# Cached K of an attention layer laid out in DRAM during the layer before it, and loaded in one transfer of 8 KB rows

## The chip, the cores and the metric

The kernel runs on one core of one Trainium2 chip. A core has a matrix engine (TensorE, PE in the profile, with PEld for its weight loads), a vector engine (VectorE, DVE), a scalar engine (ScalarE, ACT), a general engine (GpSimd, POOL) and a sync engine (SyncE, SP) that here issues nearly all DMAs. Each engine runs its instructions in the order in which they stand in its own queue, and waits at an instruction until what it needs is there. The core has 16 DMA engines, an on-chip memory of 128 partitions (SBUF) and eight accumulation banks (PSUM) of 128 x 512 floats. The metric is the device time of one execution in microseconds (us), as the median of several runs.

## What is computed

Two transformer-like layers over 512 prompt tokens and 8 x 16 sample tokens (640 in all), in float32. Layer 0 is a gated MLP with a spatial mix over blocks of 128 tokens, layer 1 is an attention with 16 heads of width 128 and a forget bias. The 8 sample sequences of layer 1 also attend to 256 cached rows each, which come as `cache_fox_k` and `cache_fox_v` in DRAM. Cut to that:

```python
for i in range(2):
    hp, hs = rms_norm(xp, norm_pre[i]), rms_norm(xs, norm_pre[i])
    if i == 0:                       # gated MLP: u, v, z = h @ w_in (1024 x 6144)
        ...                          # y = gelu(u) * (w_s mixes layer_norm(gelu(v))) * silu(z); y @ w_out
    else:                            # q, k, v, z, logf = h @ w_in (1024 x 8208)
        op = (fox_attend_prompt(qp, kp, vp, lfp) * silu(zp)) @ fox_w_out
        att_s = fox_attend_sample(qs, ks_, vs_, lfs, cache_fox_k, cache_fox_v, cache_fox_logf)
        os_ = (att_s * silu(zs)) @ fox_w_out
    xp, xs = xp + rms_norm(op, norm_post[i]), xs + rms_norm(os_, norm_post[i])
    ...                              # gated embedding input added to xp and xs

def fox_attend_sample(q, k_new, v_new, logf_new, k_cache, v_cache, logf_cache):
    k = jnp.concatenate([k_cache, k_new], axis=1)          # (8, 256 + 16, 16, 128)
    v = jnp.concatenate([v_cache, v_new], axis=1)
    s = jnp.einsum('bqhd,bkhd->bhqk', q, k) * scale        # + forget bias, causal mask, softmax
    return jnp.einsum('bhqk,bkhd->bqhd', p, v)
```

`cache_fox_k` holds 8 x 256 x 16 x 128 floats (16.8 MB).

## The kernel before, in words

**Precision.** Each float32 product is made of three passes of the matrix engine. `split` (L261) makes a high part on ACT (L263) and a low part on DVE (L264); `mm3` (L247) issues high x high, high x low and low x high (L249 to L251). Every weight and every activation goes through such a split.

**Weights.** A list of units of 512 KB each is fetched in order by SP into a ring of three buffers, `RAW` (and in part of layer 0 a fourth one in `R1`). `weights` (L224) and `prefetch` (L201) split units into the ring `W`, which has five places, as far ahead as places are free. A fetch waits until the split of the unit that used its buffer is done, and a split waits until PE is done with the place in `W`.

**Layer 0.** First four panels of the v part (L434): sixteen units, each for 30 matmuls of 512 columns. Then eight pairs of channel groups (L588), g = 0, 2, ... 14. For each pair `seven_products` (L523) runs twice, for u and for z. It forms a 2 x 2 block product with seven block products in place of eight; POOL prepares sums of weights (L198), DVE and ACT add up the seven results out of four PSUM banks (L528, L536 to L543), ACT and DVE apply gelu and the gate (L578, L582, L583). At the end of a pair `gate_spatial` (L557) mixes v along the tokens (L565, L566) and multiplies (L568, L570, L573), and then calls `spatial_weights` (L494) for the group two further on. That issues three small loads of 64 KB each: the mixing matrix `w_s` (L497), its bias `b_s` copied to all partitions (L498), and a row of sums `rs_sc` (L499), written once to DRAM before. The bias and the sums go into buffers that the group two before has just been reading, so they can be issued only when L568 and L570 of that group are done. L500 on DVE combines these two loads as soon as they are there; its result is first read by L568 of that later group. Layer 0 ends with `tail` (L602): 16 units of the output product, then the embedding.

**Layer 1.** For each of 8 head pairs p the projections v, k, q, z (L846 to L894) run on PE, and pieces of the attention of the pair before are put between them by `interleave` (L328), which takes a list of (due time, piece) and issues a piece when the sum of the projection steps reaches its due time. The cached rows are handled in 16 sets (p, bg), bg being the half of the 8 sample sequences. `load_k` (L974) loads one set of cached K: 8 DMAs of 128 KB that bring rows of 32 floats (128 bytes) so that each of four partition quarters holds 32 x 32 blocks. `turn_k` (L987) then transposes these blocks on DVE (L992, eight instructions) into `kt`, and `scores` (L1009) multiplies them (L1014). Set (p, 1) is loaded at due time 2 of a pair and set (p + 1, 0) in the middle of it; the transposes of a set come some 22 us later. One buffer of 1 MB (`o_K` in `r2b_t`) takes all sets in turn.

**What sets the order.** A scheduler places the instructions of each engine from the program order, the data they wait for and its own estimate of times; `queued` (L122) asks that what follows be issued right behind a given instruction. So an added DMA can also move instructions on DVE, ACT and PE.

Of the kernel before, what the change touches and what calls it, by code (L numbers as in the profile page):

```python
# [17 lines left out]
F32 = mybir.dt.float32  # L18
# [6 lines left out]
P = 128  # L25
# [32 lines left out]
def hybrid_trunk(tc, x_prompt, x_sample, ck, cv, clf, p_prompt, p_sample, norm_pre, norm_post,  # L58
# [25 lines left out]
    x_sc = dram.tile([NT, P, D], F32, name="x_sc")  # L84
    y_sc = dram.tile([H, P, TOK], F32, name="y_sc")
    c_sc = dram.tile([H, SEQ], F32, name="c_sc")
    cs_sc = dram.tile([P, 272], F32, name="cs_sc")
    rs_sc = dram.tile([16, P], F32, name="rs_sc")

# [28 lines left out]
    def dma(out, in_):  # L118
        behind["sp"] = nc.sync.dma_start(out=out, in_=in_)
# [104 lines left out]
    def weights(n):  # L224

        i0 = state["used"]
        state["used"] += n
        prefetch(i0 + 2 * NW, i0)
        res = []
        for i in range(i0, i0 + n):  # L230
            u, j = items[i]
            k, o, m = units[u][1], place[i][0] * 1024, len(place[i]) * 512
            if j in (1, 2):
                views = [W[:, o + z:o + z + m].rearrange("p (a k n) -> p k a n", a=2, k=k) for z in (0, m)]
            else:
                views = [W[:, o + z:o + z + m].rearrange("p (k n) -> p k n", k=k) for z in (0, m)]
            res.append(tuple(views))
        return res
# [8 lines left out]
    def mm3(out, lhs, rhs, start, stop):  # L247
        (lh, ll), (rh, rl) = lhs, rhs
        nc.tensor.matmul(out, lh, rh, start=start, stop=False)  # L249
        nc.tensor.matmul(out, lh, rl, start=False, stop=False)  # L250
        nc.tensor.matmul(out, ll, rh, start=False, stop=stop)  # L251
# [50 lines left out]
    def h_at(k, a, b):  # L302
        return h_hi[:, k, a:b], h_lo[:, k, a:b]
# [38 lines left out]
    def r2(o, n, p=P):  # L342
        return R2[:p, o:o + n]
# [64 lines left out]
                split(*right_sum(dst), o)  # L408


    def v_at(p, t):
        return r1(p * 2560 + t * 512, 512)

# [20 lines left out]
    for p in range(4):  # L434
        if p == 2:
            with queued("act", "dve", "sp"):
                spatial_constants()
        out = [bank((0, 1, 2, 3, 4, 5, 6, 7)) for _ in range(NT)]
        for kk in range(4):
            (w,) = weights(1)  # L440
            for t in range(NT):
                for j in range(2):
                    k = 2 * kk + j
                    mm3(out[t], h_at(k, t * P, (t + 1) * P), (w[0][:, j], w[1][:, j]), k == 0, k == 7)
            if (p, kk) == (1, 1):
                with queued("act", "dve"):
                    right_operands()
            if (p, kk) == (3, 1):
                split(*quarter(0, 1), b12)
        for t in range(NT):  # L450
            behind["act"] = nc.scalar.activation(out=v_at(p, t), in_=out[t], func=AF.Gelu_apprx_tanh)
            behind["dve"] = nc.vector.bn_stats(out=stats[t][:, 6 * p:6 * p + 6], in_=v_at(p, t))
# [58 lines left out]
    def uv_of(g):  # L511
        return r1(o_u + (g % 2) * TOK, TOK), r1(o_tz + (g % 2) * TOK, TOK)
# [10 lines left out]
    def seven_products(into, done):  # L523

        rights = (quarter(0, 0), right_sum(1), quarter(0, 1), right_sum(0), quarter(1, 1), quarter(1, 0), right_sum(2))

        def total(i, j, a, b):
            nc.vector.tensor_tensor(out=into(i, j), in0=a, in1=b, op=ALU.add)  # L528
            done(i, j, into(i, j))

        for n, (w, right) in enumerate(zip(seven_left(), rights)):
            o = bank(UZ)[:, :HT]
            for k in range(4):
                mm3(o, (w[0][:, k], w[1][:, k]), (right[0][:, k], right[1][:, k]), k == 0, k == 3)
            if n == 0:
                nc.scalar.activation(out=m1, in_=o, func=AF.Copy)  # L536
            elif n == 1:
                nc.vector.tensor_tensor(out=u2, in0=m1, in1=o, op=ALU.add)  # L538
            elif n == 2:
                nc.vector.tensor_tensor(out=u3, in0=u2, in1=o, op=ALU.add)  # L540
            elif n == 3:
                total(1, 1, u3, o)
                nc.vector.tensor_tensor(out=u2, in0=u2, in1=o, op=ALU.add)  # L543
            elif n == 4:
                total(0, 1, u2, o)
            elif n == 5:
                total(0, 0, m1, o)
            else:
                total(1, 0, u3, o)
# [38 lines left out]
    for g in range(0, 16, 2):  # L588
        for part, finish in ((0, finish_u), (1, finish_z)):
            if 2 * part in SEVEN:  # L590
                seven_products(lambda i, j: uv_of(g + i)[part][:, HALF[j]], lambda i, j, c: finish(g, i, j, c))
            else:
                eight_products(lambda i, j, c: finish(g, i, j, c))
        if g < 6:

            with queued("act", "dve"):
                layer_norm_panel(1 + g // 2)
        for i in range(2):
            gate_spatial(g + i)


    def tail(layer, y_at, first_banks, attention=None):  # L602
# [3 lines left out]
        last = layer == 1  # L606
# [39 lines left out]
        def out_steps(h, kks):  # L646
            out = [PB[i] for i in halves[h]]
            for kk in kks:
                (w,) = weights(1)

                split_y(min(2 * kk + 4, 14) if attention and h == 0 and kk < 7 else 16 * h + 2 * kk + 6)
                if h == 1 and kk == 2 and last:
                    embedding_input((2, 3, 4))
                if h == 1 and kk == 5:
                    for t in range(NT):
                        dma(x1[t], tok_rows(xin_p, xin_s, t) if not last else x_sc[t])
                for t in range(NT):
                    for j in range(2):
                        g = 2 * kk + j
                        i, ts = 16 * h + g, slice(t * P, (t + 1) * P)  # L660
                        mm3(out[t], (y_part(i, 0)[:, ts], y_part(i, 1)[:, ts]), (w[0][:, j], w[1][:, j]), g == 0, g == 15)
                    yield 1.36
# [95 lines left out]
    n = NT * H  # L758
# [207 lines left out]
    def kv_of(p, bg):  # L966

        i = 2 * p + bg
        kr = r2(o_K, 2048).rearrange("p (h b n) -> p h b n", h=2, b=4)
        kt = r2(o_KT, 2176).rearrange("p (h b k) -> p h b k", h=2, b=4)  # L970
        vv = [r2(o_V + (2 * i + z) % 3 * 1024, 1024).rearrange("p (b t n) -> p b t n", b=2, t=2) for z in range(2)]
        return kr, kt, vv

    def load_k(p, bg):  # L974
        kr, _, _ = kv_of(p, bg)
        for hh in range(2):
            for qd in range(4):
                d = slice(qd * 32, (qd + 1) * 32)
                dma(kr[d, hh].rearrange("p b (c d) -> p (b c) d", d=32),
                    ck[0, 4 * bg:4 * bg + 4, :, 2 * p + hh, d].rearrange("b (c j) d -> j (b c) d", j=32))  # L980

    def load_v(p, bg):
        for z, vv in enumerate(kv_of(p, bg)[2]):
# [161 lines left out]
```

## Time and profile before

| | |
|---|---|
| median of 3 runs | 1334.27 us (1334.1 to 1334.35) |
| the profiled execution | 1334.83 us, of which 1333.0 us is the span of the profile |
| granted PE clock | 0.999 |
| busy time of PE | 1321.0 us |
| busy time of DVE, ACT, POOL | 766.4, 542.9, 135.7 us |
| moved by DMA | 172.87 MB in 299913 packets, 188769 of them under 512 bytes |
| share of DMA engine time in use | 0.3 to 0.4 from 67 to 540 us, 0.7 to 0.8 from 540 to 1100 us |

The profile is of one execution. A busy PE means that matmuls follow each other without a gap that the records show; the ends of matmuls are modelled, so two matmuls in a row overlap in the records. "Idle before" is the time in which an engine had nothing to run, with the instruction or DMA that ended it. The chain of waits follows the last instruction back to what released it, and so on to the start. Rows with SPq are DMA issues: the time is that of the issue, not of the transfer.

Layer 0 runs to about 457 us (panels to 126 us, the pairs of groups to 347 us, then the output product), the embedding and the norm to about 540 us, layer 1 to the end, its attention part to about 1190 us.

### The profile page before, as it was taken

The page shows a single profiled execution, that of the slowest core. Times are in us where ns is not written, and L with a number is a line of the kernel's source. Part 1 is how long each engine was busy: PE and PEld are TensorE (multiplying, and loading weights), DVE is VectorE, ACT ScalarE, POOL GpSimd, SP SyncE. Part 2 cuts the span into 40 slices and gives each one's busy share as a digit, 9 for nine tenths or more (in the row PEclk, how much of TensorE's full clock was granted, in tenths as well). Part 3 has the DMA queues.
Part 4 walks back from the last instruction along what each step waited for, and adds up shares of the span by engine and source line. Part 5 has one row for each costly group of instructions (what it writes and reads, how often), then busy time and mean ns, then how long its engine had stood idle before and what let it go on. Part 6 is the DMA issues. An engine that isn't in the chain of part 4 may idle for free.

```text
span 1333.0 us, 21550 instructions
## 1 busy us (share of the span) xinstructions
PE 1321.0 (99%) x8363; PEld 1191.6 (89%) x8363; DVE 766.4 (57%) x1581; ACT 542.9 (41%) x1025; POOL 135.7 (10%) x144
## 2 busy tenths in 40 slices
PE   9999999999999999999999999999999999999998
PEld 6888999999988788999999999999999998888786
DVE  7744899998844546544545454444545465544642
ACT  5434555444535334523433333433334344435341
POOL 1013444543000100000000000000000000000100
PEclk9999999999999999999999999999999999999999
DMA  6432334232324204688778575778778687243211
GB/s 224 138 100 70 120 114 130 66 109 68 127 95 158 78 18 127 178 142 158 138 154 176 145 163 141 164 144 163 125 151 169 152 212 235 101 149 111 64 64 47
DMA packets 299913, 172.87 MB, mean 130 GB/s; under 512 B 188769, under 2 KB 269201, under 8 KB 299810
## 3 DMA queue, kind: packets, MB, share of 16 engines
q1 hardware_dynamic: 299666, 171.23, 51.7%
q8 instruction: 65, 1.06, 0.3%
q14 instruction: 38, 0.31, 0.1%
q10 hardware_dynamic: 144, 0.26, 0.1%
HBM read 149.86 MB, written 21.59 MB: 129 GB/s over the span
## 4 chain that ended last, share of the span: by engine, by line
PE 94%; DVE 3%; issue 1%; ACT 1%; DMA 0%; POOL 0%; SPq 0%; DVEq 0%
PE pb L249 28%; PE pb L251 27%; PE pb L250 27%; PE pb L960 3%; PE pb L953 1%; PE pb L1014 1%; PE pb L1040 1%; PE pb L287 1%; DVE W L264 1%; PE pb L565 1%; PE pb L1037 1%; DVE R L583 0%; DMA RAW<-in_gmlp_w_in 0%; PE pb L1032 0%; DVE R L528 0%
## 5 line engine op out<-in xcount | busy, mean ns | idle before, releaser
L249 PE MATMUL pb<-A,W 128*128 128x384 f32 (+2 forms) x1024 | 330.2, 322 | 2.1 <-DVE R L538 1.8
L251 PE MATMUL pb<-A,W 128*128 128x384 f32 (+2 forms) x1024 | 317.1, 310 | 0.0
L250 PE MATMUL pb<-A,W 128*128 128x384 f32 (+2 forms) x1024 | 316.6, 309 | 0.0
L249 PE MATMUL pb<-W,A 128*128 128x512 f32 (+1 forms) x840 | 298.3, 355 | 2.1 <-ACT R L686 1.4
L251 PE MATMUL pb<-W,A 128*128 128x512 f32 (+1 forms) x840 | 293.7, 351 | 0.6 <-DVE A L264 0.6
L250 PE MATMUL pb<-W,A 128*128 128x512 f32 (+1 forms) x840 | 294.0, 350 | 0.0
L264 DVE TENSOR_TENSOR W<-RAW,W 128x1024 fp32r<-128x1024 f32 (+1 forms) x156 | 194.0, 1244 | 139.7 <-ACT W L263 137.5
L263 ACT ACTIVATE W<-RAW 128x1024 fp32r<-128x1024 f32 (+1 forms) x156 | 161.1, 1033 | 156.8 <-PE pb L250 65.1
L249 PEld LDWEIGHTS pb<-A,W 128*128 128x128 f32 x1024 | 193.0, 188 | 10.9 <-issue 6.8
L250 PEld LDWEIGHTS pb<-A,W 128*128 128x128 f32 x1024 | 193.0, 189 | 0.6
L251 PEld LDWEIGHTS pb<-A,W 128*128 128x128 f32 x1024 | 192.6, 188 | 0.4 <-issue 0.4
L249 PEld LDWEIGHTS pb<-W,A 128*128 128x128 f32 x840 | 159.1, 189 | 26.4 <-issue 3.1
L251 PEld LDWEIGHTS pb<-W,A 128*128 128x128 f32 x840 | 158.9, 189 | 21.1 <-DVE A L264 0.9
L250 PEld LDWEIGHTS pb<-W,A 128*128 128x128 f32 x840 | 159.0, 189 | 20.4 <-issue 0.4
L264 DVE TENSOR_TENSOR A<-R,A 128x640 fp32r<-128x640 f32 (+1 forms) x51 | 41.0, 835 | 74.1 <-ACT A L263 71.9
L992 DVE STREAM_TRANSPOSE r2b_t<-r2b_t 128x256 f32<-128x256 f32 x128 | 46.4, 413 | 33.9 <-PE pb L1014 26.2
L263 ACT ACTIVATE A<-R 128x640 fp32r<-128x640 f32 (+1 forms) x51 | 36.6, 746 | 67.7 <-PE pb L250 65.7
L249 PE MATMUL pb<-tb,W 128*128 128x320 f32 x192 | 59.8, 312 | 0.1
L251 PE MATMUL pb<-tb,W 128*128 128x320 f32 x192 | 59.5, 310 | 0.0
L250 PE MATMUL pb<-tb,W 128*128 128x320 f32 x192 | 59.5, 310 | 0.0
L273 POOL TENSOR_TENSOR SML<-SML 128x1 f32<-128x1 f32 x25 | 18.1, 724 | 385.1 <-DVE SML L271 380.5
L955 ACT ACTIVATE R<-pb 128x128 f32<-128x128 f32 (+1 forms) x64 | 27.9, 436 | 65.7 <-PE pb L953 65.4
(235 smaller groups left out, 1866.7 us busy)
## 6 DMA issues: line engine op xcount, KB each, us to landing
RAW<-in_fox_w_in SPq DMA_DIRECT2D x64, 512.0 KB
RAW<-in_gmlp_w_in SPq DMA_DIRECT2D x40, 512.0 KB
r2b_t<-in_cache_fox_v SPq DMA_DIRECT2D x32, 512.0 KB
r2b_t<-in_cache_fox_k SPq DMA_DIRECT2D x128, 128.0 KB
RAW<-in_gmlp_w_out SPq DMA_DIRECT2D x16, 512.0 KB
RAW<-in_ple_w_gate SPq DMA_DIRECT2D x16, 512.0 KB
RAW<-in_fox_w_out SPq DMA_DIRECT2D x16, 512.0 KB
out<-R SPq DMA_DIRECT2D x40, 128.0 KB
```

Source lines behind the costliest of these rows:

```text
L249: nc.tensor.matmul(out, lh, rh, start=start, stop=False)
L250: nc.tensor.matmul(out, lh, rl, start=False, stop=False)
L251: nc.tensor.matmul(out, ll, rh, start=False, stop=stop)
L263: nc.scalar.activation(out=hi, in_=src, func=AF.Copy)
L264: nc.vector.tensor_tensor(out=lo, in0=src, in1=f(hi), op=ALU.subtract)
L273: nc.gpsimd.tensor_tensor(out=q, in0=t, in1=mhalf, op=ALU.pow)
L287: nc.tensor.transpose(out=b[:, j * P:(j + 1) * P], in_=src[:, (4 * c + j) * P:(4 * c + j + 1) * P], identity=ident)
L565: nc.tensor.matmul(b0[:, t * P:(t + 1) * P], v_at(pnl, t)[:, c0:c0 + P], wm, start=True, stop=True)
L953: nc.tensor.transpose(out=tb[:, j * P:(j + 1) * P], in_=pr[:, j * P:(j + 1) * P], identity=ident)
L955: nc.scalar.activation(out=pt[:, :n], in_=tb[:, :n], func=AF.Copy)
L960: nc.tensor.matmul(O[:, d], v[:, j, hh * P:(hh + 1) * P], pt[:, j * P:(j + 1) * P], start=(j == 0), stop=(j == i))
L992: nc.vector.transpose(out=kt[:, hh, bl, :PAST], in_=kr[:, hh, bl])
```

## The change

A DRAM buffer `kc_sc` of 16 sets of 1 MB is added. During layer 0, 128 DMAs copy the cached K from DRAM to this DRAM buffer in the order in which the transposes want it: each is one of the old 128 KB loads with its 128-byte pieces, but with DRAM as the target. They are issued on SP right behind the last DMA issued at that place: two behind each of the 16 weight units of the panels, four behind each of the 16 calls of `seven_products`, two behind each of the 16 units of the output product. In layer 1 `load_k` becomes one DMA of 1 MB, 128 rows of 8 KB, in place of eight of 128 KB.

```diff
+    kc_sc = dram.tile([16, P, 2048], F32, name="kc_sc")
...
+    laid = iter([(p, bg, hh, qd) for p in range(8) for bg in range(2) for hh in range(2) for qd in range(4)])
+
+    def lay_k(n):
+        with queued("sp"):
+            for _ in range(n):
+                p, bg, hh, qd = next(laid)
+                d = slice(qd * 32, (qd + 1) * 32)
+                dma(kc_sc[2 * p + bg, d, hh * 1024:(hh + 1) * 1024].rearrange("j (n d) -> j n d", d=32),
+                    ck[0, 4 * bg:4 * bg + 4, :, 2 * p + hh, d].rearrange("b (c j) d -> j (b c) d", j=32))
...                                   # panels, in the loop over the units
+            lay_k(2)
...                                   # pairs of groups, once for u and once for z
                 seven_products(lambda i, j: uv_of(g + i)[part][:, HALF[j]], lambda i, j, c: finish(g, i, j, c))
+                lay_k(4)
...                                   # output product of layer 0, in the loop over the units
+                if not last:
+                    lay_k(2)
...
     def load_k(p, bg):
-        kr, _, _ = kv_of(p, bg)
-        for hh in range(2):
-            for qd in range(4):
-                d = slice(qd * 32, (qd + 1) * 32)
-                dma(kr[d, hh].rearrange("p b (c d) -> p (b c) d", d=32),
-                    ck[0, 4 * bg:4 * bg + 4, :, 2 * p + hh, d].rearrange("b (c j) d -> j (b c) d", j=32))
+        dma(r2(o_K, 2048), kc_sc[2 * p + bg])
```

Lines of the changed kernel stand 1 lower up to L410 of before, 13 lower in `spatial_weights`, `seven_products` and `gate_spatial` (L500 is L513 there, L538 is L551, L540 is L553, L568 is L581).

How the instructions stand, first on SP in the middle of layer 0, where the pair g = 2, 3 ends and the loads for groups 4 and 5 are issued. Before (`RAW` is a weight fetch; `in_gmlp_b_s`, `rs_sc` and `in_gmlp_w_s` are the three small loads of `spatial_weights`):

```order
L119 DMA sf<-rs_sc 128x128
L119 DMA R_69<-in_gmlp_w_s 128x128
L119 DMA RAW<-in_gmlp_w_in 128x4x256 x2
L119 DMA R_69<-in_gmlp_b_s 128x128
L119 DMA R_69<-rs_sc 128x128
L119 DMA R_69<-in_gmlp_w_s 128x128
L119 DMA R_69<-in_gmlp_b_s 128x128
```

The same place now:

```order
L120 DMA sf<-rs_sc 128x128
L120 DMA R_69<-in_gmlp_w_s 128x128
L120 DMA RAW<-in_gmlp_w_in 128x4x256
L120 DMA kc_sc<-in_cache_fox_k 32x32x32 x4
L120 DMA RAW<-in_gmlp_w_in 128x4x256
L120 DMA R_69<-in_gmlp_b_s 128x128 x2
L120 DMA R_69<-rs_sc 128x128
```

Four copies now stand between the two weight fetches, ahead of both bias loads and of the sums. One pair later (end of g = 4, 5) it is alike: two weight fetches and then four copies stand ahead of the bias load for group 7, which stood ahead of the fetches before, and of the bias load and the sums for group 8. And again at the end of g = 6, 7 and the middle of the next pair, for groups 9 and 10, before

```order
L119 DMA R_69<-rs_sc 128x128
L119 DMA R_69<-in_gmlp_b_s 128x128
L119 DMA RAW<-in_gmlp_w_in 128x4x256 x2
L119 DMA R_69<-in_gmlp_w_s 128x128
L119 DMA sf<-rs_sc 128x128
L119 DMA R_69<-in_gmlp_b_s 128x128
```

and now:

```order
L120 DMA R_69<-rs_sc 128x128
L120 DMA R_69<-in_gmlp_b_s 128x128
L120 DMA RAW<-in_gmlp_w_in 128x4x256 x2
L120 DMA kc_sc<-in_cache_fox_k 32x32x32 x4
L120 DMA R_69<-in_gmlp_b_s 128x128
L120 DMA sf<-rs_sc 128x128
```

The last two loads, for group 10, stand behind the four copies here.

On DVE the scheduler has put L500 (now L513) a few instructions later in most of these places. At the first of the three, before (`W<-sf`, `W<-R` are low parts of splits, `pb` are PSUM banks):

```order
L264 TENSOR_TENSOR W<-sf,W 128x1024
L500 SCALAR_TENSOR_TENSOR sf<-sf,SML,R_69 128x128
L568 SCALAR_TENSOR_TENSOR R_69<-pb_76,SML,sf 128x4x128
L500 SCALAR_TENSOR_TENSOR R_69<-R_69,SML 128x128
L264 TENSOR_TENSOR W<-R_69,W 128x512
L538 TENSOR_TENSOR R_69<-R_69,pb_72 128x320
L540 TENSOR_TENSOR R_69<-R_69,pb_73 128x320
```

and now:

```order
L265 TENSOR_TENSOR W<-sf,W 128x1024
L265 TENSOR_TENSOR W<-R_69,W 128x512
L551 TENSOR_TENSOR R_69<-R_69,pb_72 128x320
L513 SCALAR_TENSOR_TENSOR sf<-sf,SML,R_69 128x128
L513 SCALAR_TENSOR_TENSOR R_69<-R_69,SML 128x128
L553 TENSOR_TENSOR R_69<-R_69,pb_73 128x320
```

A split and L538 moved ahead of the two L500, and L568 between them moved away to a later place. The order on PE changes only in layer 0, where some two dozen matmuls, most of them of the spatial mix, move past their neighbours; in layer 1 it is the same as before.

## The prediction

> **What bounds the kernel now.** I read the page first, then busy time by stretches, the waits of PE, the chain of waits, and the timelines of DVE and SP where the chain leaves PE.
>
> ```profile
> PE 1321.0 (99%) x8363; PEld 1191.6 (89%) x8363; DVE 766.4 (57%) x1581; ACT 542.9 (41%) x1025; POOL 135.7 (10%) x144
> ```
>
> PE is idle for 12 us in the whole span. By stretches (columns: length, busy time of PE, PEld, DVE, ACT, POOL, clock, share of the DMA engines' time, GB/s):
>
> ```profile
> 540.00:610.00 70.00, 70.00 (x498) 66.43 (x497) 29.35 (x56) 24.86 (x43) 3.45 (x6) 1.00 0.82 162
> 610.00:800.00 190.00, 190.00 (x1473) 180.14 (x1472) 95.99 (x302) 69.76 (x160) 5.30 (x18) 1.00 0.76 155
> 800.00:1000.00 200.00, 200.00 (x1544) 189.88 (x1543) 94.17 (x284) 73.44 (x165) 4.58 (x15) 1.00 0.73 148
> ```
>
> Where the cached K is loaded today the DMA engines work at 0.73 to 0.82 of their time, but PE is busy in all of it. The waits of PE between 540 and 1212 us have no row at all. So no transfer of layer 1 ends a wait of PE, and a shorter or earlier one has nothing to give back there.
>
> Layer 0 is different in its pairs of groups:
>
> ```profile
> 177.00:200.00 23.00, 23.00 (x161) 22.53 (x160) 22.72 (x34) 11.78 (x24) 11.17 (x7) 1.00 0.34 101
> 200.00:222.00 22.00, 21.59 (x149) 21.15 (x148) 20.09 (x31) 13.23 (x23) 8.11 (x6) 1.00 0.35 108
> 222.00:259.00 37.00, 36.26 (x248) 35.62 (x247) 34.24 (x52) 16.67 (x31) 18.07 (x11) 1.00 0.35 106
> 259.00:277.00 18.00, 17.01 (x120) 16.82 (x118) 17.33 (x25) 8.82 (x16) 7.85 (x5) 1.00 0.26 81
> ```
>
> DVE is busy 22.72 of 23 us and 17.33 of 18 us, as full as PE. The chain of waits in order of time (start, length, what) says which of the two binds:
>
> ```profile
> 177.61 0.48 DVE R L540
> ...
> 181.35 1.84 DVE W L264
> ...
> 200.53 0.48 DVE R L528
> ...
> 259.34 1.45 issue
> ...
> 275.92 0.74 DVE R L559
> ```
>
> From 177.6 to 201 us and from 259 to 277 us it runs mostly over DVE. The waits of PE between 166 and 300 us name the link, L538, which empties a PSUM bank that PE needs:
>
> ```profile
> PE pb L249 <- DVE R L538: 1.8, 2, 1.1
> ```
>
> So **layer 1 is bound by PE alone, and from 177 to 277 us layer 0 has DVE and PE both full**, with next to no reserve between them. Here the change puts its copies.
>
> **What it removes in layer 1: nothing on the path.** 128 loads go, each holding SP for 562 ns at the median:
>
> ```profile
> L119 SPq DMA_DIRECT2D r2b_t<-in_cache_fox_k x128: 317/562/3949, 567.7 to 1090.0; - x128
> ```
>
> Only DVE waited for them visibly, in two places (L992; us in all, times, longest):
>
> ```profile
> DVE r2b_t L992 <- DMA r2b_t<-in_cache_fox_k: 6.3, 2, 3.8
> ```
>
> DVE has half its time free there (95.99 of 190 us busy). Gain: 0. The 1 MB load that takes their place must wait for all eight transposes of the set before, not for four, and lands as a whole. At the 155 GB/s of this stretch it takes 1.05 MB / 155 = 6.8 us, and the transposes come some 22 due-time us later. The first set, which is transposed at 574 us today, moves to about 585 us in the order. Cost: 0, covered by those 22 us; if the cover went, DVE would wait with half its time free.
>
> **What it adds in layer 0.** A copy from DRAM to DRAM is not in the trace. The nearest rows are 128-byte loads from DRAM and 128-byte stores to DRAM (the K rows of the new tokens):
>
> ```profile
> 570.00:572.00 2.00, 2.00 (x9) 0.67 (x7) 0.36 (x1) 0.00 (x0) 0.00 (x0) 1.00 0.98 148
> 573.80:575.20 1.40, 1.40 (x12) 1.40 (x11) 1.02 (x3) 0.76 (x1) 0.00 (x0) 1.00 0.56 82
> ```
>
> The first is mostly loads: 148 / 0.98 = 151 GB/s with the engines full, so 131072 B take 0.87 us. The second is all stores: 82 / 0.56 = 146 GB/s, 0.90 us. A copy reads and writes such pieces. If both sides overlap it costs 0.87 us, if one follows the other 1.77 us; from below, 0, if it fits wholly into gaps. I take 0.87 us, the nearest row, and a group of four as **3.5 us**, and keep 0 and 7 us for the range.
>
> In the panels and in the output product two copies (1.7 us) come per weight unit, and a unit is 30 matmuls, by the count below 30 x 33.00 / 149 = 6.6 us of PE. The stretch, then SP's waits (fetches wait for buffers, not for the transfer):
>
> ```profile
> 34.00:67.00 33.00, 33.00 (x149) 27.31 (x148) 25.74 (x22) 13.27 (x15) 0.23 (x2) 1.00 0.47 143
> ```
>
> ```profile
> SPq L119 <- DVE W L264: 316.0, 75, 31.1
> ```
>
> ACT's waits show only five for a fetch of layer 0's w_in; its timeline has the first and the last of them within 20 us, for the first five fetches, and in the new order all copies stand behind these:
>
> ```profile
> ACT W L263 <- DMA RAW<-in_gmlp_w_in: 5.7, 5, 3.5
> ```
>
> ```profile
> 7.70 1.06 ACT L263 ACTIVATE W<-RAW 128x1024 fp32r<-128x1024 f32 x1 [3.52 <-DMA RAW<-in_gmlp_w_in]
> ...
> 19.64 1.06 ACT L263 ACTIVATE W<-RAW 128x1024 fp32r<-128x1024 f32 x1 [0.19 <-DMA RAW<-in_gmlp_w_in]
> ```
>
> Cost: 0, covered by the five places of `W` (some 30 us of PE); without that, 1.7 us per unit.
>
> In the pairs of groups the weights are as well covered, but **the small loads are not**. L500 on DVE already waits for them in three places (DVE, with the wait and its cause; then SP):
>
> ```profile
> 175.04 0.35 DVE L500 SCALAR_TENSOR_TENSOR sf<-sf,SML,R 128x128 f32<-128x128 f32 x1 [1.55 <-DMA R<-in_gmlp_b_s]
> 177.61 0.49 DVE L540 TENSOR_TENSOR R<-R,pb 128x320 f32<-128x320 f32 x1
> ...
> 205.84 0.35 DVE L500 SCALAR_TENSOR_TENSOR sf<-sf,SML,R 128x128 f32<-128x128 f32 x1 [1.46 <-DMA sf<-rs_sc]
> 206.72 0.48 DVE L538 TENSOR_TENSOR R<-R,pb 128x320 f32<-128x320 f32 x1
> 207.30 0.49 DVE L540 TENSOR_TENSOR R<-R,pb 128x320 f32<-128x320 f32 x1
> ...
> 234.60 0.35 DVE L500 SCALAR_TENSOR_TENSOR sf<-sf,SML,R 128x128 f32<-128x128 f32 x1 [1.61 <-DMA R<-in_gmlp_b_s]
> 234.87 0.48 DVE L538 TENSOR_TENSOR R<-R,pb 128x320 f32<-128x320 f32 x1
> ...
> 235.86 1.22 DVE L264 TENSOR_TENSOR W<-sf,W 128x1024 fp32r<-128x1024 f32 x1
> ```
>
> ```profile
> 168.11 1.50 SPq L119 DMA_DIRECT2D RAW<-in_gmlp_w_in  x2
> 169.70 0.46 SPq L119 DMA_DIRECT2D R<-in_gmlp_b_s  x1
> ...
> 199.33 0.38 SPq L119 DMA_DIRECT2D RAW<-in_gmlp_w_in  x1
> 202.10 0.33 SPq L119 DMA_DIRECT2D R<-in_gmlp_b_s  x1
> 202.76 0.33 SPq L119 DMA_DIRECT2D sf<-rs_sc  x1
> ...
> 227.68 1.47 SPq L119 DMA_DIRECT2D RAW<-in_gmlp_w_in  x2
> ```
>
> A small load is served behind what was issued before it: alone it is used 205.84 - 202.76 = 3.1 us after its issue, behind two fetches 175.04 - 169.70 = 5.3 us. From the issue of the second fetch (169.2, being 168.11 + 1.50 - 0.38; 228.8 likewise) to the use it is 5.8 us both times. In the new order four copies stand there too, so that the data come 5.8 + 3.5 = 9.3 us after the second fetch. The 2.2 us for which SP issues the copies lie inside that.
>
> - Place 1: data at 169.2 + 9.3 = 178.5; two L500 (0.27 us each, as from 234.60 to 234.87) end at 179.05. L540, next in the new order, started at 177.61: **1.45 us late**. A split and L538 now run ahead of L500, which the waiting hides.
> - Place 2: 199.33 + 9.3 = 208.6; then L500, L538 and L500, some 0.95 us, so L540 at 209.55 and not at 207.30: **2.25 us late**.
> - Place 3: 228.8 + 9.3 = 238.1, L500, then the split at 238.35 and not at 235.86: **2.5 us late**.
>
> At the other L500 of layer 0 the order puts L500 later than 9.3 us behind the second fetch, or no copies stand just ahead. Sum on DVE: 6.2 us. Of that PE is spared what DVE has free. From 200 to 222 us DVE is idle for 1.91 us, 1.46 of it the wait above, so 0.45 is free; from 222 to 259 us 2.76 less 1.61, so 1.15. At place 1 nothing is: the chain runs over DVE right there. So PE ends 1.45 + 1.8 + 1.35 = **4.6 us** later, and nothing after 277 us gives it back, since PE is full. That is 1334.83 + 4.6 = 1339.4 us for the profiled execution, and on the median, 0.56 us lower, **1338.9 us**.
>
> **The Trainium skill against the trace.** "DMA: Bandwidth & Descriptors", section "Why small descriptors are slow (HBM only)", gives each packet about 3 cycles on top of one per 32 bytes; for 128 bytes that makes 4/7 of the 435 GB/s of the section "Where 436 GB/s comes from", an estimate of 249 GB/s, 2.1 us per group of four and by rival 1 below 0.4 us on PE: no change. The load row above, 151 GB/s with the engines full, speaks against it. The section "Specifications" of that page says that below 512 bytes the engine does a read-modify-write, so a write would cost a read too, as in the second rival below. The store row, 146 GB/s, shows no such surcharge on stores from SBUF; no row here shows a write from DRAM.
>
> **The rivals.**
> 1. *The small loads come hardly later, and the new order wins.* Were the copies free, L500 moved behind work that is ready would shed the three waits of 1.55 + 1.46 + 1.61 = 4.6 us; PE could take back at most its idle time from 200 to 277 us, 0.41 + 0.74 + 0.99 = 2.1 us: 1332.2 us. In general DVE loses 3 x (group) less 4.3 us (6.2 at 3.5) and PE 1.6 less. So it turns at a group of 2.0 us, and up to 2.9 us it stays within 0.2% (2.7 us, about what a measurement of this kernel can tell from no change). For it: only 0.35 of the DMA time is used there. Against it: the queue rows.
> 2. *Read and write one after the other:* 7 us per group, 3 x 7 - 4.3 - 1.6 = 15.1 us, 1349 us, and up to 1356 us with three more L500 (160, 276, 300 us) that would then wait. Against it: load and store rows that are alike.
> 3. *Faster, by less traffic in layer 1.* Matmuls of 512 columns took 391 ns on average from 350 to 457 us and 395 ns from 1130 to 1200 us, where more is moved:
>
> ```profile
> L249 PE MATMUL pb<-W,A 128*128 128x512 f32 x157 | 61.4, 391 | 0.0
> ```
>
> ```profile
> L249 PE MATMUL pb<-W,A 128*128 128x512 f32 x83 | 32.8, 395 | 0.0
> ```
>
>  If DMA writes were the cause of that 1%, the 540 us of K loading could win as much at most: 5.4 us, 1328.9 us. Against it: ends of matmuls are modelled, and 4 ns is little.
> 4. *It doesn't do what it says:* a 1 MB load lands late and the transposes wait. DVE has room, so 1334.3 us.
>
> **How the numbers follow.** Forecast (a group of 2.9 to 5 us) 0.50, own range 1337 to 1343; rival 2 0.12; rival 1 with all that stays within 0.2%, and rival 4, together 0.33; rival 3 0.05. That makes slower by over 0.2% 0.62, same 0.33, faster 0.05. The range from 1332.5 (rival 1) to 1349 (rival 2 at its three places) leaves out rival 3 and the upper part of rival 2.
>
> **What would show it.** L513 of the new profile waits about 3 to 4 us for `b_s` or `rs_sc` at the three places, PE's waits for L551 grow from 1.8 to some 6 us between 170 and 280 us, and layer 1 keeps its length. If L513 doesn't wait longer, the copies are cheaper than 0.5 us each; waits of 7 us would mean the double price. A shorter layer 1 with a full PE would show rival 3; new waits of PE after 570 us for transposes, rival 4.

## The result, and the profile after

| | before | after |
|---|---|---|
| median (4 runs each, the same chip) | 1334.19 us (1334.1 to 1334.35) | 1342.91 us (1342.27 to 1343.39) |
| the profiled execution, its span | 1334.83, 1333.0 us | 1342.27, 1340.5 us |

The ratio is 1.0063, with a 95% interval of 1.0051 to 1.0076: 8.7 us slower, where 4.6 were forecast. The busy times of the page of after are almost those of before:

```profile
PE 1322.6 (99%) x8363; PEld 1191.6 (89%) x8363; DVE 765.5 (57%) x1581; ACT 542.3 (40%) x1025; POOL 133.4 (10%) x144
```

PE works 1.6 us longer and is idle for 18 us in place of 12. Layer 1 (windows, columns as in the prediction) moves about as many GB/s in less DMA time, with PE as full as before:

```profile
610.00:800.00 190.00, 190.00 (x1475) 180.14 (x1475) 92.97 (x284) 71.36 (x159) 3.72 (x16) 1.00 0.60 150
800.00:1000.00 200.00, 200.00 (x1540) 190.92 (x1539) 96.83 (x297) 72.13 (x163) 3.94 (x17) 1.00 0.61 152
```

The share of DMA time falls from 0.76 and 0.73 to 0.60 and 0.61, and nobody gains by it. The lost time lies in the pairs of groups. DVE's waits there from 120 to 350 us (us, times, longest):

```profile
DVE R L513 <- DMA R<-in_gmlp_b_s: 8.1, 3, 4.5
DVE sf L513 <- DMA sf<-rs_sc: 6.3, 3, 4.7
DVE sf L513 <- DMA R<-in_gmlp_b_s: 3.4, 1, 3.4
```

That is 17.8 us in seven waits, where before there were 5.4 us in four, three of them of about 1.5 us. PE's waits between 170 and 280 us, 7.1 us in all against 2.1 before, are for DVE and ACT to empty PSUM banks:

```profile
PE pb L250 <- DVE R L541: 2.5, 2, 1.3
PE pb L250 <- DVE R L551: 2.1, 3, 0.8
PE pb L250 <- ACT R L549: 1.5, 2, 1.1
PE pb L250 <- DVE R L556: 1.0, 2, 0.6
```

The timeline of DVE shows the three places that the prediction named, and behind them two waits (at 284.91 and 341.53 us) that it did not expect:

```profile
177.79 0.35 DVE L513 SCALAR_TENSOR_TENSOR sf<-sf,SML,R 128x128 f32<-128x128 f32 x1 [3.39 <-DMA R<-in_gmlp_b_s]
178.28 0.35 DVE L513 SCALAR_TENSOR_TENSOR R<-R,SML 128x128 f32<-128x128 f32 x1
178.55 0.48 DVE L553 TENSOR_TENSOR R<-R,pb 128x320 f32<-128x320 f32 x1
...
209.98 0.35 DVE L513 SCALAR_TENSOR_TENSOR R<-R,SML 128x128 f32<-128x128 f32 x1 [4.50 <-DMA R<-in_gmlp_b_s]
...
211.69 0.35 DVE L513 SCALAR_TENSOR_TENSOR sf<-sf,SML,R 128x128 f32<-128x128 f32 x1 [0.96 <-DMA sf<-rs_sc]
211.95 0.48 DVE L553 TENSOR_TENSOR R<-R,pb 128x320 f32<-128x320 f32 x1
...
243.31 0.35 DVE L513 SCALAR_TENSOR_TENSOR sf<-sf,SML,R 128x128 f32<-128x128 f32 x1 [4.72 <-DMA sf<-rs_sc]
243.58 1.22 DVE L265 TENSOR_TENSOR W<-sf,W 128x1024 fp32r<-128x1024 f32 x1
...
284.91 0.35 DVE L513 SCALAR_TENSOR_TENSOR R<-R,SML 128x128 f32<-128x128 f32 x1 [1.70 <-DMA R<-in_gmlp_b_s]
...
341.53 0.35 DVE L513 SCALAR_TENSOR_TENSOR R<-R,SML 128x128 f32<-128x128 f32 x1 [1.85 <-DMA R<-in_gmlp_b_s]
```

To see how much of that PE pays, I cut both traces at the same points of the program. All kernels make the 112 block products of the pairs in the same order, so the start of the first matmul of the 28th, 37th, 49th, 67th and 79th product marks one point in each. At the 49th it is this row of PE's timeline, before and after:

```profile
225.88 0.39 PE L249 MATMUL pb<-tb,W 128*128 128x320 f32 x1
```

```profile
230.49 0.39 PE L250 MATMUL pb<-tb,W 128*128 128x320 f32 x1
```

So PE is 4.61 us late there. The windows between the cuts, before and after:

```profile
180.95:201.06 20.11, 19.98 (x140) 19.32 (x139) 20.08 (x30) 10.51 (x24) 10.06 (x6) 1.00 0.42 129
201.06:225.88 24.82, 23.79 (x163) 23.28 (x164) 22.91 (x35) 14.27 (x24) 8.53 (x6) 1.00 0.35 106
225.88:258.46 32.58, 32.58 (x223) 32.20 (x222) 29.87 (x45) 15.07 (x29) 17.19 (x11) 1.00 0.32 97
258.46:282.49 24.03, 22.94 (x161) 22.75 (x159) 23.20 (x34) 10.52 (x20) 10.86 (x7) 1.00 0.21 67
```

```profile
180.26:202.85 22.59, 20.80 (x142) 19.58 (x141) 22.41 (x35) 13.02 (x26) 11.36 (x7) 1.00 0.56 139
202.85:230.49 27.64, 24.52 (x167) 23.38 (x166) 21.86 (x33) 13.03 (x23) 8.89 (x6) 1.00 0.57 138
230.49:266.13 35.64, 33.07 (x222) 32.10 (x221) 29.30 (x44) 15.00 (x27) 17.11 (x11) 1.00 0.48 117
266.13:290.24 24.11, 23.21 (x161) 22.77 (x160) 22.06 (x34) 10.26 (x21) 10.56 (x7) 1.00 0.52 112
```

The first three stretches, each with one of the places in it or just ahead of it, take 2.48, 2.82 and 3.06 us longer, the fourth 0.08. Less the 0.69 us by which after was ahead at the first cut that makes 7.75 us, and the span is 7.5 us longer. The whole loss is there; layer 1 neither gains nor loses. The waits of 1.70 and 1.85 us at 284.91 and 341.53 us cost PE nothing: the first lies in the fourth stretch, and at the start of the last product, the 112th (345.67 us before, 353.44 now), PE is still 7.8 us late and no more.

### The profile page after: what moved, and what is told of

The parts are those of the page before. It is cut to its first block, busy times and chain, and to the rows that moved or that the text cites. A ratio compares the mean times of both kernels' runs of the same rounds, so it can differ in the third digit from the quotient of the medians.

```text
span 1340.5 us, 21502 instructions
## 1 busy us (share of the span) xinstructions
PE 1322.6 (99%) x8363; PEld 1191.6 (89%) x8363; DVE 765.5 (57%) x1581; ACT 542.3 (40%) x1025; POOL 133.4 (10%) x144
## 4 chain that ended last, share of the span: by engine, by line
PE 91%; DVE 5%; issue 1%; DMA 1%; SPq 1%; ACT 1%; POOL 0%; DVEq 0%
PE pb L250 27%; PE pb L252 26%; PE pb L251 26%; PE pb L976 3%; DVE W L265 2%; PE pb L969 1%; PE pb L1025 1%; PE pb L1051 1%; PE pb L288 1%; SPq L120 1%; DVE R L596 1%; PE pb L578 1%; DVE R L541 1%; PE pb L1048 1%; DMA sf<-rs_sc 1%
## 5 line engine op out<-in xcount | busy, mean ns | idle before, releaser
L1004 POOL COPY r2b_t<-R 128x64 f32<-128x64 f32 x32 | 8.7, 270 | 489.9 <-PE pb L1025 438.1
```

## The experiments

Ratios are against the kernel before, run on the same chip beside them, with 95% intervals; the expectations were written before the runs. After the twelve runs a table gives the stretches of those on which the argument rests.

**No copies in the pairs of groups.**

```diff
-            lay_k(2)                  # panels
+            lay_k(4)
...
-                lay_k(4)              # behind the calls of seven_products
...
-                    lay_k(2)          # output product
+                    lay_k(4)
```

> All 128 copies are kept, but none stands in the pairs of groups: four per weight unit in the panels and four per unit of the output product. The order on PE and ACT is that of the kernel before. Theory A (the copies ahead of the small loads make L513 wait, and nothing else costs): 1334.2 us, at most 1335, L513 waits as L500 did before (1.5 us at three places), span 7.5 us shorter than that of the changed kernel. Rival B (the new order that the scheduler gives to the spatial mix costs): also 1334.2, since that order is gone. Rival C (copying 16.8 MB costs wherever it stands, by traffic or by the time of SP): 1340 to 1343 us. Four copies per unit take 3.5 us beside a fetch of about 3 us and 6.6 us of PE, so if the cover of the panels is thinner than I took it, ACT's waits for w_in grow there and the time is up to 1338.

1335.41 us, ratio 1.0004 (0.9995 to 1.0013). L513 waits 1.49, 1.33 and 1.79 us at the three places, as L500 did. Rival C falls: the time shows nothing of the 128 copies, though twice as many as before the edit stand in the panels. One small load is late there too: the last four copies of the panels stand ahead of a load for the layer norm, DVE (L489) waits 2.64 us for it at 133.68 us, and the first nine products of the pairs take 0.3 us longer.

**Copies behind the u call only, or the z call only.** The prediction had left open whether late data or the scheduler's new order costs. These two kernels part them.

```diff
-                lay_k(4)
+                lay_k(4 - 4 * part)   # u only; in the second kernel 4 * part: z only
```

The other 32 copies go to the panels and the output product, three per unit.

> In the pairs the four copies stand behind the u call only (32 copies there, the other 32 in the panels and the output product). These are the ones that stand ahead of the bias loads and the sums at 168, 200 and 233 us. The order on PE and ACT is that of the kernel before, on DVE only L513 moves back by two or three instructions. Theory A (late data): L513 waits 3 to 5 us at the three places as in the changed kernel, 1341 to 1343 us. Rival B (order of the spatial mix): 1334 to 1335. Half and half: 1338.

> The other half: in the pairs the four copies stand behind the z call only, where no bias load or sums follow within some 5 us at the three places. The order on PE and ACT is exactly that of the changed kernel. Theory A (late data): no wait of L513 over 2 us, 1334 to 1335.5 us. Rival B (the order of the spatial mix costs by itself): 1341 to 1343 us, with PE waits for L551 and L541 as in the changed kernel but no long wait of L513.

U only: 1342.41 us, ratio 1.0056 (1.0044 to 1.0069). Z only: 1333.19 us, ratio 0.9986 (0.9977 to 0.9995). DVE's timeline of the u kernel has the long waits:

```profile
178.21 0.35 DVE L513 SCALAR_TENSOR_TENSOR sf<-sf,SML,R 128x128 f32<-128x128 f32 x1 [3.35 <-DMA R<-in_gmlp_b_s]
...
211.51 0.35 DVE L513 SCALAR_TENSOR_TENSOR sf<-sf,SML,R 128x128 f32<-128x128 f32 x1 [4.21 <-DMA sf<-rs_sc]
...
243.80 0.35 DVE L513 SCALAR_TENSOR_TENSOR sf<-sf,SML,R 128x128 f32<-128x128 f32 x1 [5.33 <-DMA sf<-rs_sc]
```

and that of the z kernel has shorter ones, though two of them are over the 2 us that theory A allowed:

```profile
176.68 0.35 DVE L513 SCALAR_TENSOR_TENSOR sf<-sf,SML,R 128x128 f32<-128x128 f32 x1 [2.71 <-DMA R<-in_gmlp_b_s]
...
206.95 0.35 DVE L513 SCALAR_TENSOR_TENSOR R<-R,SML 128x128 f32<-128x128 f32 x1 [2.01 <-DMA R<-in_gmlp_b_s]
...
235.83 0.35 DVE L513 SCALAR_TENSOR_TENSOR sf<-sf,SML,R 128x128 f32<-128x128 f32 x1 [1.44 <-DMA R<-in_gmlp_b_s]
```

The old order on PE with long waits has the whole loss, the new order with shorter waits has none in the end. Late weights are not the cause, though weight fetches stand behind the copies too: in the u kernel ACT, which splits the fetches of layer 0, waits for none of them from 126 to 355 us. One thing was not expected: the z kernel does lose time at place 1. Its windows:

```profile
180.76:202.92 22.16, 20.54 (x143) 19.59 (x141) 21.98 (x34) 12.93 (x26) 10.91 (x7) 1.00 0.57 140
202.92:227.28 24.36, 23.61 (x168) 23.34 (x166) 21.92 (x33) 13.02 (x23) 8.56 (x6) 1.00 0.50 134
227.28:259.67 32.39, 32.39 (x222) 32.07 (x221) 29.33 (x44) 15.10 (x27) 17.17 (x11) 1.00 0.42 113
259.67:282.71 23.04, 23.04 (x161) 22.77 (x160) 22.11 (x34) 10.28 (x21) 10.58 (x7) 1.00 0.39 97
```

DVE is full in the first stretch and is busy 1.9 us longer in it than before (21.98 against 20.08); 2.05 us are lost. Two things push work into it: the new order (L568, at 175.50 us before and so ahead of the cut, is L581 at 196.18 us here) and a longer wait at place 1 (2.71 us for 1.55), behind which L553 starts at 178.59 us where L540 started at 177.61. A later run parts them: the z kernel with the small loads earlier (below) has the new order too, but waits only 1.56 us at place 1, its L553 (L557 there) starts at 177.13 us, and its first stretch is 0.56 us longer. So most of the z kernel's 2.05 us goes with the longer wait, and under 1 us with the order. Of the loss 0.46, 0.19 and 0.99 us come back in the next stretches.

**Layer 1 alone.** No copies; each set comes in one load straight from the cache as it lies there, so the cached keys are in a wrong order.

```diff
-        dma(r2(o_K, 2048), kc_sc[2 * p + bg])
+        dma(r2(o_K, 2048), ck[0].rearrange("b c h d -> (b c h d)").rearrange("(s p n) -> s p n", s=16, p=P)[2 * p + bg])
```

> No copy at all; layer 1 loads each set of K in one transfer of 1 MB, 128 rows of 8 KB, straight out of the cached K in the order in which it lies there, so the attention to cached rows is computed from keys in a wrong order. It has the loads of the changed layer 1 without the copies. Theory A (layer 1 is bound by PE alone): 1334.2 us, within 0.7. Rival D (less traffic and fewer issues in layer 1 are worth something): 1329 to 1332.5. If the one late transfer per set costs: over 1335, with waits of PE after 570 us.

1334.83 us, ratio 0.9997 (0.9988 to 1.0006), no wait of PE between 540 and 1212 us. Of the 1.7 to 5.2 us that rival D gave to less traffic, nothing is there.

**Two copies in place of four.**

```diff
-                lay_k(4)
+                lay_k(2 - 2 * part)
```

The other copies go to the panels, four per unit, and the output product, three per unit.

> As copies_behind_u_only, with two copies in place of four behind each u call; the rest goes to the panels and the output product. The order on PE and ACT is that of the kernel before. A group is now 1.75 us at the price of the prediction. Four copies cost 7.9 us of PE at the three places, 10.5 us of copy time. Theory A1 (PE loses what the group exceeds a small cover by, the same at each place: 3 x (3.5 - t) = 7.9, t = 0.9 us): 3 x (1.75 - 0.9) = 2.6 us, 1336.8. Theory A2 (in proportion, no cover at all): 4.0 us, 1338.2. Theory A3 (the prediction: 6.2 us of lateness on DVE, of which 1.6 us are spared and the turn is at a group of 2 us): no loss, 1334.2.

1338.90 us, ratio 1.0034 (1.0021 to 1.0046). The waits of L513 are 1.86 and 0.61, 2.05 and 4.04 us, and the three stretches lose 3.57 us. Another 0.9 us goes in the first nine products of the pairs, where the copies of the panels delay the load for the layer norm (DVE waits 2.70 us at L489, at 134.59 us, as in the kernel without copies in the pairs, where it cost 0.3 us). A3, the rule of the prediction, falls. The 3.57 us lie between A1 and A2, nearer to A2: about in proportion, with little cover.

**Copies in rows of 4 KB.** The cached keys are again in a wrong order.

```diff
-                dma(kc_sc[2 * p + bg, d, hh * 1024:(hh + 1) * 1024].rearrange("j (n d) -> j n d", d=32),
-                    ck[0, 4 * bg:4 * bg + 4, :, 2 * p + hh, d].rearrange("b (c j) d -> j (b c) d", j=32))
+                i = p * 16 + bg * 8 + hh * 4 + qd
+                dma(kc_sc[2 * p + bg, d, hh * 1024:(hh + 1) * 1024],
+                    ck[0].rearrange("b c h d -> (b c h d)").rearrange("(s j n) -> s j n", s=128, j=32)[i])
```

> The changed kernel with each copy of 128 KB as 32 rows of 4 KB, in the order in which they lie in the cache, so the attention to cached rows is computed from keys in a wrong order. Copies stand at the same places as in the changed kernel, the order on PE and ACT is that of the kernel before. Theory G (a copy's price goes by its 128-byte pieces): at the rate at which the weight fetches beside them move, about 310 GB/s in pieces of 1 KB, a copy takes 0.42 us and a group 1.7 us; SP issues the four in under 2.5 us: 1335.5 to 1338 us, as with two copies. Rival H (the price goes by bytes written to DRAM, or by the number of DMAs ahead of the small loads): 1341 to 1343 us.

1338.18 us, ratio 1.0025 (1.0014 to 1.0035): half of the loss in the three stretches with all the bytes, so the pieces make half the price, G rather than H, just above what G said. With two fetches beside them the copies fill the DMA engines (window of this kernel):

```profile
203.00:205.00 2.00, 2.00 (x15) 2.00 (x14) 1.97 (x6) 1.93 (x4) 0.00 (x0) 1.00 0.99 336
```

This is the rate of both together: of the 534 packets in this window 55 are 4 KB pieces of the copies, a third of the bytes. By it a copy takes some 131072 / 336 = 0.39 us and a group of four 1.6 us, an estimate, like two copies in small pieces (1.7 us by the rate below). The three stretches lose 4.06 us.

**Small loads in ACT's queue.**

```diff
-        dma(r1(o_bs + z * P, P), b_s[0, g].partition_broadcast(P))
-        dma(spb[z], rs_sc[g].partition_broadcast(P))
+        nc.scalar.dma_start(out=r1(o_bs + z * P, P), in_=b_s[0, g].partition_broadcast(P))
+        nc.scalar.dma_start(out=spb[z], in_=rs_sc[g].partition_broadcast(P))
```

> The changed kernel, all copies where it has them, but the bias load and the sums of a group are issued on ACT and so stand in another DMA queue than the copies. The order on PE is that of the changed kernel. Theory E (they are late because they stand behind the copies in SP's queue, in issue and in service): L513 waits 2 us at most, 1334 to 1336 us. Rival F (they are late because the DMA engines themselves are full of copies, whatever the queue): L513 still waits 3 to 5 us at the three places, 1340 to 1343 us. ACT gets some 30 issues of 0.35 us; that is covered, with ACT busy 542 of 1340 us, unless it waits at one for the buffer: then 1337 or more, with PE waits for ACT.

1337.77 us, ratio 1.0021 (1.0012 to 1.0030). The time lies between the ranges of E and F. No wait of L513 is over 1.96 us, as E said, though at place 2 it waits twice (1.96 and 1.81 us). A third of the loss in time is left, and half of that in the three stretches. Of their 4.2 us 2.01 are place 1, as in the z kernel, whose PE order this one has but for two rows. The rest is not settled. A small load issued by ACT at 202.38 us has landed at 207.20, 4.8 us later, against 2.8 us for one at 197.35 before the copies start, so a part of F holds too. The time also fits an ACT that waits at an issue (1337 or more), but the sign of it is missing: PE waits 1.4 us for ACT (L549), against 1.5 in the changed kernel.

**Z only, with the small loads in ACT's queue**: both edits together.

> copies_behind_z_only with the bias load and the sums issued on ACT: a try at a version that beats both kernels. Without copies or fetches of the same queue ahead of them the small loads should come about 3 us after their issue, and the waits of 1.5 to 2.7 us of L513 go. Theory A: PE idles some 11 us in the whole kernel, about 2 us of it in the pairs of groups, so 1332 to 1333.5 us. If DVE's waits there were covered anyway: 1333.2 to 1334.2, the same as copies_behind_z_only. If ACT waits at an issue for the buffer: over 1335.

1334.79 us, ratio 1.0001 (0.9992 to 1.0010). L513 still waits up to 2.1 us, since the loads must wait for their buffers and then take some 3 us. No gain over z alone, nor over the kernel before: theory A falls.

**Small loads a pair of groups earlier**, with four buffers each for the bias and the sums, in the space of a table of layer 1 that is loaded later. Three kernels: on the changed kernel, on the kernel before, and on the z kernel.

```diff
+    spb = ..., CST[:, C_TRI:C_TRI + P], CST[:, C_TRI + P:C_TRI + 2 * P]
+    def spatial_loads(g):
+        dma(bsb[g % 4], b_s[0, g].partition_broadcast(P))
+        dma(spb[g % 4], rs_sc[g].partition_broadcast(P))
...                                   # end of gate_spatial
+        if g + 4 < 16:
+            spatial_loads(g + 4)
         if g + 2 < 16:
             spatial_weights(g + 2)
```

> The changed kernel with all its copies where they are, but four buffers for the bias and four for the sums in place of two (the space is that of a table of layer 1, loaded after layer 0 instead), and both loads of a group issued one pair earlier. The order on PE is that of the changed kernel but for some 20 rows. Theory A (nothing but late data costs): no wait of L513 for them in the pairs, and the loss at 207 and 236 us (2.7 and 3.2 us of PE) goes; the 2 us that the new order took at 185 to 201 us by itself with the copies behind z may stay: 1333 to 1336 us. If the copies also delay something else in the pairs (weights): 1338 or more.

> The kernel before, without any copy, with the same four buffers and loads one pair earlier. It takes away the three waits of 1.5 us that L500 had already. If DVE's wait costs PE from its first microsecond (no cover): 1332 to 1333 us, since PE idles 2.3 us between 181 and 282 us before. If waits of 1.5 us are covered: 1334.2, the same. The order on PE changes in 450 rows of layer 0, so up to 2 us either way may come from that.

> copies_behind_z_only with the four buffers and the loads one pair earlier: a second try at a version that beats both kernels. 1332 to 1334 us; the gain over the kernel before can be 2.3 us at most, which PE idles in the pairs of groups there.

The first missed by far: 1348.37 us, ratio 1.0098 (1.0084 to 1.0111). Its DVE timeline has the waits where they were (L517 is L513 here):

```profile
177.83 0.83 DVE L517 SCALAR_TENSOR_TENSOR CST<-CST,SML 128x128 f32<-128x128 f32 x2 [3.33 <-DMA CST<-in_gmlp_b_s]
...
211.34 0.35 DVE L517 SCALAR_TENSOR_TENSOR R<-R,SML 128x128 f32<-128x128 f32 x1 [5.84 <-DMA R<-in_gmlp_b_s]
...
244.44 0.35 DVE L517 SCALAR_TENSOR_TENSOR sf<-sf,SML,R 128x128 f32<-128x128 f32 x1 [5.14 <-DMA sf<-rs_sc]
```

Two more waits follow, at 286.19 us (1.84 us) and at 317.38 us (2.84 us); the second costs 2.8 us of PE, between the 91st and the 103rd product. The rows that wait are now those for two groups later: the scheduler brought the combining instruction forward with its loads, to where it reckoned them done, still behind the copies on SP. So the data are a pair early, but so is the instruction that blocks DVE for them, and the test of "the data in time" was not made by it. The same edit without copies gave 1334.57 us, ratio 0.9998 (0.9989 to 1.0007), with waits of 1.5 us left near places 2 and 3 and one of 3.50 us at 287.42 us: it tells little on cover at the three places. On the z kernel it gave 1332.86 us, ratio 0.9985 (0.9976 to 0.9994).

**Z only once more.**

> copies_behind_z_only once more, beside the others of this call, since its ratio of 0.9986 stood against a span that was 0.2 us longer than that of the kernel before. If the gain is real: a ratio of 0.998 to 0.999 again. If the profile is right: 1.000, 1333.5 to 1335 us.

1333.68 us, ratio 0.9988 (0.9980 to 0.9997). The intervals of three runs of z kernels (z only, once more, and with early loads) lie below 1, by 0.03 to 0.24%: a gain of some 1.5 to 2 us over the kernel before, at the edge of what can be told. That of the fourth, with ACT's queue, does not. Where the gain comes from is not shown in full. In all four the second and the fourth stretch are shorter than before, and the wait at place 1 takes that back, or does not (table). The fourth stretch of the first z kernel above runs without PE idle, where 1.1 us of idle stood; but its profiled execution is the slowest of its eleven (1335.03 us) and has no gain in all, and in that of the second PE is 0.5 us ahead at the 112th product, of 1.1 us in the span.

Extra time of PE in each stretch against before, in us, worked out from the starts of the marked products, and group time (copies times bytes over the measured rate):

| kernel | group | 1 | 2 | 3 | 1 to 3 | 4 |
|---|---|---|---|---|---|---|
| no copies in pairs | 0 | 0.21 | -0.13 | 0.16 | 0.2 | -0.06 |
| z only | 0 at the places | 2.05 | -0.46 | -0.19 | 1.4 | -0.99 |
| z only once more | 0 at the places | 1.90 | -0.87 | -0.18 | 0.9 | -1.05 |
| z only, early loads | 0 at the places | 0.56 | -0.86 | -0.10 | -0.4 | -0.85 |
| z only, ACT's queue | 0 at the places | 1.78 | -0.34 | 0.25 | 1.7 | -1.25 |
| 4 KB rows | 1.6, estimate | 1.49 | 0.67 | 1.90 | 4.1 | -0.06 |
| u only, two | 1.7 | 1.00 | 0.39 | 2.18 | 3.6 | 0.00 |
| u only, four | 3.3 | 1.71 | 2.52 | 3.73 | 8.0 | -0.06 |
| the change | 3.3 | 2.48 | 2.82 | 3.06 | 8.4 | 0.08 |
| ACT's queue | 3.3, other queue | 2.01 | 1.14 | 1.01 | 4.2 | -1.25 |

## Why the prediction was right, and what was too small

- **Layer 1 gains nothing and loses nothing: right.** Shown by the run of layer 1 alone and by the run without copies in the pairs. Rivals 3 and 4 fall with it.
- **Copies in the panels and the output product cost nothing: right** for the changed kernel. With four per unit it holds but for the layer norm's load at the end of the panels, which cost 0.3 and 0.9 us in two runs.
- **A copy costs 0.87 us: right.** While only copies run (all packets are under 512 bytes), the changed kernel shows

```profile
207.00:208.00 1.00, 1.00 (x9) 1.00 (x8) 0.00 (x0) 0.63 (x1) 0.00 (x0) 1.00 0.99 157
```

  that is 131072 / 157 = 0.83 us, 3.3 us for the group, as fast as a load alone (151 GB/s). Reading and writing overlap, so rival 2 (7 us) falls. The Trainium skill's overhead per packet ("DMA: Bandwidth & Descriptors", "Why small descriptors are slow (HBM only)") had made 249 GB/s, an estimate; that is too fast by a factor of 1.6. The section "Specifications" there puts a read-modify-write below 512 bytes. Copies in pieces of 128 bytes do move at less than half the rate of copies in 4 KB rows with fetches beside them (157 against 336), but no run parts that rule from an overhead per piece.
- **Three places where L513 waits for small loads: right**, at 177.8, 210 and 243.3 us, and they hold all of the loss. That no other L513 would wait longer was wrong (1.70 us at 284.91, 1.85 at 341.53), but these waits cost nothing.
- **The terms of the sum were too small: 4.6 us forecast, 7.75 in the trace.** Step by step:
  - *"The 2.2 us for which SP issues the copies lie inside that", and so "9.3 us after the second fetch"*: this failed. SP's timeline of the changed kernel at place 2:

```profile
199.23 1.19 SPq L120 DMA_DIRECT2D RAW<-in_gmlp_w_in  x2
200.47 6.19 SPq L120 DMA_DIRECT2D kc_sc<-in_cache_fox_k  x4
206.77 1.06 SPq L120 DMA_DIRECT2D R<-in_gmlp_b_s  x2
208.19 0.33 SPq L120 DMA_DIRECT2D sf<-rs_sc  x1
```

    The issue of four copies takes 6.19 us (4.8 and 5.2 at the other places), not 2.2, and the small loads are issued only then. The row from which the 2.2 us came, 317/562/3949 ns, showed single issues of up to 3.9 us; only its median was used. From there the bias is used after 3.2 us (206.77 to 209.98) and the sums after 3.5 (208.19 to 211.69), like a load alone before (3.1). From the second fetch (199.23 + 1.19 - 0.38 = 200.04) that makes 9.9 and 11.65 us, and 9.9 at place 3. On DVE, L553 starts at 211.95 us and not at 207.30, 4.65 us late, of which 1.79 were there at the cut before it (202.85 for 201.06): place 2 adds 2.86 us, where 2.25 were forecast. At place 3 the split starts at 243.58 and not at 235.86, 7.72 us late, 4.61 of them from before: 3.11 us for 2.5. PE loses 2.82 and 3.06 us there, 0.57 and 0.56 more than the forecast lateness.
  - *"Of that PE is spared what DVE has free", 1.6 us*: nothing was spared. At places 2 and 3 the lateness (2.86 and 3.11 us) went to PE whole (2.82 and 3.06). With group times of 1.6 to 1.7 us, below the forecast turn of 2.0, PE already loses 3.6 to 4.1 us, and with 3.3 us 8.0: about 2.1 to 2.6 us per us of group time, out of three. PE was full in the third stretch before (32.58 of 32.58 us), so what DVE makes good later does not come back to PE; in the second it had 1.03 us of idle, and those did not help either. Why the waits at 284.91 and 341.53 us were covered all the same was not tested.
  - *Place 1, 1.45 us*: 2.48 in the trace. L553 stands at 178.55 us, even earlier than forecast (179.05). What I left out is that L568, moved "away to a later place" (from 175.50 to 196.12 us), is still to be done on a full DVE: after was 0.69 us ahead at the first cut and then had 22.41 us of DVE work for 20.08. The kernels of the other runs give it a size. At the second cut PE of the changed kernel is 1.79 us late, its L553 0.94 us (178.55 for 177.61): 0.85 us more. In all seven kernels with the new order PE is there 0.85 to 0.89 us later than L553 was, also where L553 comes 0.48 us early (z only with early loads); in the five with the old order it is as late as L553 within 0.05 us (u only: 1.96 and 1.92); the kernel with early loads and no copies has an order of its own there (0.5). So PE loses the whole lateness at this place too, and the new order costs 0.87 us by itself.
  - So: 4.6 + 1.6 (not spared) - 0.51 (L553 0.94 us late, not 1.45) + 0.85 (the new order) + 0.57 + 0.56 (the longer waits at places 2 and 3) + 0.08 (the fourth stretch) = 7.75 us. The 0.69 us of lead are in the 0.85.
  - That the time still lies in "own range 1337 to 1343" is in part luck. The range was meant for dearer copies (a group of up to 5 us); with the group as measured, 3.3 us, the rule of the prediction gives 3 x 3.3 - 4.3 - 1.6 = 4.0 us, 1338.3 us. The copies cost what was forecast, and the rest of the 8.7 us came by the terms above.
- **"What would show it": half right.** Waits of 3 to 4 us were 3.4 to 4.7. PE's waits grew, to 7.1 us, but spread over L541, L551, L549 and L556 rather than at L551.
- **Rival 1 (the new order wins)** is not what the z kernels show, though three of their four runs are 1.5 to 2 us faster, about the 2.1 us that it was given as a most: the waits of L513 that it would shed are still there (2.71, 2.01 and 1.44 us). What decides between loss and no loss is the queue ahead of the small loads at the three places.

## What to carry to other kernels

Ahead of putting background DMAs into a stage whose engines are full, list the small loads that stand behind them in the same queue, and count the issue time of many-piece DMAs as well as their transfer: the same copies cost 8 us behind one call and nothing behind the next. An engine's free time in a stretch is not by itself a reserve against a stall: at places 2 and 3 the engine that it feeds lost the whole stall, though at 285 and 341 us stalls of 1.7 and 1.85 us were covered. Price the whole stall first, and look for cover place by place. And traffic removed from a stage in which PE never waited was worth nothing here, however large its share of DMA time was.

## What the runs showed that I had not expected

SP's issue of one DMA can be held for more than 2 us with no semaphore to wait for. At the three places four copies of 1024 pieces each take 4.8 to 6.2 us to issue behind a fetch, four of 32 rows of 4 KB 2.4 to 2.9 us. With only two copies the hold falls on the next DMA, a small load:

```profile
201.76 1.73 SPq L120 DMA_DIRECT2D kc_sc<-in_cache_fox_k  x2
204.10 2.00 SPq L120 DMA_DIRECT2D R<-in_gmlp_b_s  x1
```

That is 2.00 us for an issue that takes 0.33 elsewhere. It looks as if the queue takes in only so many pieces ahead; no run here was made to measure how many. The Trainium skill ("Perfetto Trace Analysis", "DMA Instruction — HWDGE (DVE, Sync)") says that the issuing engine is free only once all descriptors of its DMA have been generated, and that the engines start early when the descriptor buffer fills up; the long issues agree with the first, and no row here shows the second. Its "DMA: Bandwidth & Descriptors", "Issuing engines are not separate DMA queues", calls the time on the issuing engine usually small against the DMA: here it was 6.19 us for 3.3 us of transfer, behind two fetches that were still to be moved.
